# Two loads and a few casts moved behind a named neighbour, in a hybrid decoder block

## The chip, the cores and the metric

The program runs on one core of a Trainium2 chip. The metric is the device time of one execution in microseconds (us), as the median of several runs; the profile is one further execution, taken by the hardware profiler. The core has a matrix engine (TensorE; PE in the profile, with PEld for its weight loads), VectorE (DVE), ScalarE (ACT), GpSimd (POOL) and SyncE (SP), which here does nothing but issue DMA transfers. Each engine works through its instructions in the order written in the program and waits on semaphores for the others.

## The reference

One decoder block on x of 1024 tokens by 1024 channels: a state-space branch and a forgetting-attention branch read one normalised input; they are gated and joined; then cross-attention into 256 memory tokens, and a gated feed-forward network (FFN).

```python
u = rms_norm(h, norm_mix); proj = u @ w_in            # u_ssm, q, k, v, f_logit, gate_logits
y_ssm = gelu(s5_ssm(u_ssm, ...))
glu_a, glu_b = split(y_ssm @ w_glu);  out_a = glu_a * sigmoid(glu_b)
att   = forgetting_attention(q, k, v, f_logit + b_forget)    # 8 heads of 64, causal
out_b = att @ w_fox_o
h = h + (gate_a * out_a + gate_b * out_b) @ w_mix_out
h = h + memory_cross_attention(rms_norm(h), rms_norm(mem), w_mem_q, w_mem_kv, w_mem_o)
f_a, f_b = split(rms_norm(h) @ w_ffn_in)                     # hidden width 2816
h = h + (silu(f_a) * f_b) @ w_ffn_out
return rms_norm(h, norm_final)
```

## The kernel before, in words

Every matrix product is made of three: an operand is split into a high part (`hi`, a cast on ACT, L177) and the rest (`lo`, a subtraction, mostly on DVE, L178), and hi x hi, hi x lo and lo x hi are added up in one PSUM bank. A weight thus goes through a raw slot (a DMA), a cast and a subtraction before TensorE can use it. There are two raw slots (`raw`) and four pairs of slots for the parts (`whi`, `wlo`). `B.wload` and `B.wblock` do all three steps. The large products of the tail use seven block products instead of eight (the numbers 1 to 7 in the code), so their weights are also summed before they are split.

The program is written as straight-line Python. A scheduler then sets the order in which each engine's instructions stand, by readiness, by the order written and by free slots of the pools, so an instruction may stand well ahead of its place in the code. `B.behind(ins)` (and `tc.issue_after`) holds the instructions of its block that run on the engine of `ins` behind `ins` in that engine's order. It orders the queue; it adds no wait of its own. A queue such as SP's is worked off in order: an issue that waits for a slot holds all issues behind it.

Three places matter.

**The attention (`Fox.run`).** Eight heads, each of 12 units (`scores`, `values_hi`, `values_lo`). Beside the units of head h run: the row maxima of head h+1 (`row_max`, and `max_row`, which stores them by DMA at L1722 into the row `hb`), the projection of head h+2 (`pro[h + 2].parts`, 16 pieces; for the last head 8 pieces beside head 5 and 8 beside head 6), and the load and split of the weights for head h+3 (`load`, L1652 and L1653, from `w_in`, placed behind the broadcast `spread` of the reciprocals; `split`, placed behind an exponential). So the last w_in load is issued in head 4. When a head is done, `finish` moves its denominators (`rc`, `rd_d`, `rb`) through DRAM and `divide` applies them in the next head. From the time that TensorE no longer reads the tiles of `uT`, the SSM branch's output is loaded into their slots (`load_y`, L1810). In the last head (7) the first four gated units are computed beside the units, as `filler`: for each j a load of its weights (`Glu.load`, two DMAs of 256 KB from `wg_d`, a copy of w_glu in DRAM, and a split of 128x1024), then two products (`value`).

**The first part of the tail (`stage_tail`).** For j = 0 to 7 the second half of a gated unit is finished (`glu.rest`, which loads the gate `ga`, L1211) and the attention's product for j-3 is made, multiplied by the gate `gb` and added (`fox_part`; the gate load is `load`, L555, the multiplication L587). `ga`, `gb` and others share five slots `half`; the units' outputs `sg` and others share five slots `tmp`. For j = 0 to 3 `sg` is then stored to `am_d` (L595) and its slot is free when that store has landed. `ahead(j, ...)` prepares the weights of the first two FFN tiles long before they are due: `fetch` loads two raw halves of 512 KB (`wpr`, L652), `plain`, `sums`, `seventh` and `rest` split them and store the parts to `w_d`. `ahead1` is the second tile; its raw halves use `tmp` slots, and its steps are called one by one in `side`, between the block products of the output projection (`mix_mm`, L627).

**The end of the FFN.** The first FFN product runs over 22 tiles j; for each, `start`, `middle` and `end` make the block products (`prod`, L977). `middle` ends with the copy `c1` (L998) of the bank `b1`, to which `end` then adds product 3. The second product (`o_mm`, L1114) takes its operands in pairs from DRAM: `o_get(m)` loads two halves (`or`, L1097 and L1103) and splits them, into a `whi`/`wlo` pair for m < 4 and into other slots (`oh`, `ol`) afterwards. The first four are asked for before the last `end`, three more behind it.

The order that the scheduler gives is shown below, since the code alone does not tell it.

Of the kernel before, what the change touches and what calls it, by code (L numbers as in the profile page):

```python
# [22 lines left out]
NT = 8  # L23
GRP = 32
NH = 8
# [41 lines left out]
def f32(ap):  # L67
    return ap.bitcast(F32)
# [471 lines left out]
def stage_tail(B, big, s2, sh, x, glu, aT, gate_d, kv_d, sums_d, w_fox_o, w_mix_out, g_mq, w_mem_q, w_mem_o, g_ffn,  # L540
               w_ffn_in, w_ffn_out, g_fin, out):
    nc, V, A, G, T, S, small, ident = B.nc, B.V, B.A, B.G, B.T, B.S, B.small, B.ident
# [9 lines left out]

    def load(src, name):
        t_ = sh.half(name)
        S.dma_start(t_, src)  # L555
        return t_


# [131 lines left out]
    ahead0, ahead1 = ahead(0, lambda name, dt=F32: slot(dt, name)), ahead(1, tmp)  # L690
# [43 lines left out]
    def mix_s4(kk):  # L734
        y = s2.tile([P, D], F32, tag=("xs", "gbc")[kk], bufs=1, name="s4")
        S.dma_start(y, s3_d[kk])
        for k in range(2):
            give("S4", slot, 2 * kk + k, y[:, 512 * k:512 * k + 512])

    side = [ahead1[0]] + [lambda kk=kk: mix_s4(kk) for kk in range(2)] + ahead1[1:2] + [lambda: None] + ahead1[2:3] + \  # L740
        [lambda: None] + ahead1[3:]
    mix_weights(6)
    for i in range(4):
# [245 lines left out]
    def middle(j):  # L989
        b1 = ev[j, "b1"]  # L990
        b3 = ev[j, "b3"] = B.bank("pv")
        prod(j, 6, b1, False)
        a1 = ev[j, "a1"] = sh.half("a1")
        A.copy(a1, b1)
        prod(j, 7, b3, True)
        prod(j, 5, b1, False)
        c1 = ev[j, "c1"] = sh.half("c1")
        A.copy(c1, b1)  # L998
        V.scalar_tensor_tensor(out=c1, in0=c1, scalar=-1.0, in1=b3, op0=ALU.mult, op1=ALU.subtract)

    def end(j):
# [89 lines left out]
    ops, Hf = {}, {}  # L1091
    ssq = small.tile([P, 2 * NT], F32, name="ssq", bufs=1)

    def o_get(m):
        n, p = seq[m]
        r_ = slot(name="or")
        S.dma_start(r_[:, :512], c_d[n, p])  # L1097
        if n < 4:
            j, c = 2 * p + (n > 1), 512 * (n > 2)
            src = w_ffn_out[j * P:(j + 1) * P, c:c + 512]  # L1100
        else:
            src = t_d[n, p]
        S.dma_start(r_[:, 512:], src)  # L1103
        hl = wpair(0) if m < 4 else (bslot(F32R, "oh"), bslot(F32R, "ol"))
        B.split(*hl, r_)
        ops[m] = hl

    def o_mm(m, i):
# [26 lines left out]
            S.dma_start(out[t * P:(t + 1) * P, cs], Hf[t][:, cs])  # L1135

    for m in range(4):
        o_get(m)
    end(NF - 1)
    for m in range(4, AHEAD):  # L1140
        o_get(m)
    gated(NP - 1)
    out_sums(NP - 1, 1)
    gfin = B.bcast_gain(s2, g_fin)
# [386 lines left out]
class Fox:  # L1531
# [90 lines left out]
    def setup(self):  # L1622
        fp, G = self.fp, self.B.G
        self.hb = [[self.sh.tmp("hb", F32R) if i == 0 else fp.tile([P, L], F32R, name=f"hb{s}") for s in range(4)]
                   for i in range(2)]
        for K1, K2, Q1, Q2 in self.hb:
            G.memset(f32(K1[64:69, :]), 1.0)
            G.memset(f32(Q1[64:69, :]), -1.0)

        self.tri = fp.tile([P, 512], F32, name="tri")  # L1630
        G.memset(self.tri, 0.0)
        G.affine_select(out=self.tri[:, 384:512], in_=self.tri[:, 384:512], pattern=[[-1, P]], compare_op=ALU.is_ge,
                        fill=NEG, base=0, channel_multiplier=1)
        self.trk = fp.tile([P, P], F32, name="trk")
        G.memset(self.trk, 0.0)
        G.affine_select(out=self.trk, in_=self.trk, pattern=[[1, P]], compare_op=ALU.is_ge, fill=NEG, base=0,
                        channel_multiplier=-1)
        self.pj, self.mc, self.pvs, self.num, self.rb, self.raw = {}, {}, {}, {}, {}, {}
        self.hi_todo, self.lo_todo = [], []

    def project(self, h):

# [71 lines left out]
    def max_row(self, h):  # L1714
        B = self.B
        mc = self.mc.pop(h)
        B.V.tensor_tensor(out=mc[:, 0, :], in0=mc[:, 0, :], in1=mc[:, 1, :], op=ALU.max)
        pm = B.bank("misc")
        B.T.transpose(pm[0:NT, 0:P], mc[:, 0, :], B.ident)
        mr = B.small.tile([NT, P], F32R, tag="mr", bufs=1, name="mr")  # L1720
        B.V.tensor_scalar(out=mr, in0=pm[0:NT, 0:P], scalar1=-1.0, scalar2=None, op0=ALU.mult)
        B.S.dma_start(f32(self.hb[h % 2][2][68:69, :]).rearrange("o (a b) -> o a b", a=NT), f32(mr))  # L1722

    def scores(self, h, qc, kt):
        B, fp = self.B, self.fp
# [72 lines left out]
    def run(self, y_d, yT, aT, w_glu, w_d, filler):  # L1798
        B, fp, S = self.B, self.fp, self.B.S
        self.aT = aT  # L1800
        self.prepare_v()
        for t in range(NT):
            self.values_of_v(1, t)
        self.log_forget()
        self.setup()

        def load_y(k, h):

            for i, dst in enumerate(yT.rhs(k, h)):
                S.dma_start(f32(dst).rearrange("p (t c) -> p t c", t=4),  # L1810
                            y_d[k, i, 4 * h:4 * h + 4].rearrange("t p c -> p t c"))

        def load_att(k):
            for h in range(2):
                for i, dst in enumerate(aT.rhs(k, h)):
                    S.dma_start(f32(dst), self.att_d[i, k * P:(k + 1) * P, 512 * h:512 * h + 512])

        pro = [self.project(h) for h in range(NH)]
        for h in range(2):
            loaded = pro[h].load()  # L1820
            pro[h].split()

        with B.tc.issue_after(loaded.ins):
            for k in range(4):
                S.dma_start(w_d[k].rearrange("(m g) c -> m g c", g=8),
                            w_glu[k * P:(k + 1) * P].rearrange("(g m) c -> m g c", m=16))
        for f in pro[0].parts[:8] + pro[0].evac[:1] + pro[0].parts[8:] + pro[0].evac[1:]:
            f()
        self.cumulate()
        for t in range(4):  # L1830
            self.values_of_v(0, t)
        for h in range(2):
            self.gate_rows(h)
        for f in pro[1].parts[:4]:
            f()
        weave(pro[1].parts[4:8] + pro[1].evac[:1] + pro[1].parts[8:], self.row_max(0))
        copied = pro[1].evac[1]()
        self.values_of_v(0, 4)
        self.max_row(0)
        pro[2].load()  # L1840
        pro[2].split(copied)
        pro[3].load()
        for t in range(5, 7):
            self.values_of_v(0, t)
        units = [(qc, kt) for qc in range(2) for kt in range(4 * qc + 4)]
        for h in range(NH):
            side = {i: [] for i in range(12)}
            late = h == NH - 2
            if late:
                for i, f in enumerate(pro[h + 1].parts[8:]):  # L1850
                    side[i // 2].append(f)
                side[3].append(pro[h + 1].evac[1])
            if h + 1 < NH:
                for i, f in enumerate(self.row_max(h + 1)):
                    side[(RSLOT_LATE if late else RSLOT)[i]].append(f)
                side[9].append(lambda: self.max_row(h + 1))
            if h + 2 < NH:
                n = 8 if h + 3 == NH else 16
                for i, f in enumerate(pro[h + 2].parts[:n]):
                    side[i if n == 8 else PSLOT[i]].append(f)  # L1860
                side[9].append(pro[h + 2].evac[0])
                if n == 16:
                    side[11].append(pro[h + 2].evac[1])
            if h + 3 < NH:
                side[9].append(lambda: pro[h + 3].split(self.exp))
            if h > 0 and h + 3 < NH:
                side[5].append(lambda: pro[h + 3].load(self.spread))
            if h == 0:
                side[0].append(lambda: self.values_of_v(0, 7))
            if late:  # L1870
                for k in range(8):
                    side[4 + k].append(lambda k=k: load_y(k // 2, k % 2))
            if h == NH - 1:
                for k in range(3):
                    side[6 + k].append(lambda k=k: load_att(k))
                for i, f in enumerate(filler):
                    side[i * 12 // len(filler)].append(f)
            for i, u in enumerate(units):
                self.scores(h, *u)
                for f in side[i]:  # L1880
                    f()
                if len(self.hi_todo) > 2:
                    self.values_hi()
                if len(self.lo_todo) > 1:
                    self.values_lo()
                if h and i == 4:
                    with B.tc.issue_after(self.mark.ins):
                        self.divide(h - 1)
        while self.hi_todo:
            self.values_hi()  # L1890
        while self.lo_todo:
            self.values_lo()
        self.divide(NH - 1)
# [29 lines left out]
```

## Time and profile before

| | |
|---|---|
| median of three runs | 1577.26 us (1577.14, 1577.26, 1582.96) |
| the profiled execution | 1575.91 us |
| its span, first to last instruction | 1574.2 us |
| mean granted TensorE clock | 0.992 |
| TensorE busy | 1524.9 us, 97% of the span |
| VectorE, ScalarE, GpSimd busy | 1055.2, 680.2 and 239.3 us |
| HBM read and written | 175.04 and 83.20 MB |

The times of a profile count from the start of the span. A row of a timeline gives the start, the duration, the engine, the line and the operation, with the tile written left of the arrow and the tiles read right of it; in square brackets stands how long the engine was idle just before, and what ended that. SPq and ACTq are rows of DMA issues, not of transfers. A wait row gives the total, the number of times and the longest. A row by stretch gives the busy time of each engine with the number of instructions, the granted TensorE clock as a share of full speed, the mean busy share of the DMA engines, and GB/s.

### The profile page before, as it was taken

Reading aid. Unit: us, or ns where it says so; the run is one execution under the profiler, and the core shown is the slowest. Engines: PE = TensorE matmul, PEld = TensorE weight load, DVE = VectorE, ACT = ScalarE, POOL = GpSimd, SP = SyncE. Lnnn points to the kernel's source line nnn. Section 1 sums busy time; section 2 is a strip of 40 time slices with the busy share of each in tenths; the row PEclk is TensorE's granted clock in tenths of the full one; section 3 lists DMA queues with packets and bytes.
Section 4 is the critical chain, followed back from the end, with each engine's and each line's share of the span. In section 5 each row is a group of like instructions: output and inputs, shape, how many; then the busy total and the mean of one; then the engine's idle time right before and its main releaser. Section 6 shows DMA issues by size and latency. Waiting matters only on the chain.

```text
span 1574.2 us, 20451 instructions
## 1 busy us (share of the span) xinstructions
PE 1524.9 (97%) x7261; PEld 1251.0 (79%) x7261; DVE 1055.2 (67%) x1893; ACT 680.2 (43%) x1203; POOL 239.3 (15%) x323
## 2 busy tenths in 40 slices
PE   7899999999999899999999989999999999999997
PEld 6688888898776678778788778888888888788886
DVE  5937755554777776678756687677777776565555
ACT  6523343423665653343445564333333333354342
POOL 3145342200211122210002100000000000000001
PEclk9999999999999999999999999999999999999999
DMA  8655657642124637767431186444445444896642
GB/s 255 140 134 101 185 160 154 186 131 27 35 43 69 165 113 220 245 215 265 162 107 54 67 304 243 162 154 154 158 158 164 160 159 152 286 385 217 198 148 107
DMA packets 202586, 257.66 MB, mean 164 GB/s; under 512 B 35994, under 2 KB 127034, under 8 KB 201972
## 3 DMA queue, kind: packets, MB, share of 16 engines
q1 hardware_dynamic: 195860, 240.62, 51.0%
q10 hardware_dynamic: 6624, 15.73, 2.6%
q8 instruction: 57, 0.93, 0.2%
q14 instruction: 45, 0.37, 0.1%
HBM read 175.04 MB, written 83.20 MB: 164 GB/s over the span
## 4 chain that ended last, share of the span: by engine, by line
PE 77%; DVE 8%; DMA 7%; ACT 3%; issue 2%; POOL 2%; SPq 1%; DVEq 0%; POOLq 0%; ACTq 0%
PE mm L977 15%; PE pv L977 8%; PE mm L167 6%; PE mm L168 6%; PE mm L169 6%; PE mm L1114 5%; PE sc L977 4%; PE sc L1114 4%; PE pv L1114 3%; PE sc L167 2%; PE sc L169 2%; PE sc L168 2%; PE misc L1114 2%; DMA gb<-gate_d 1%; PE mm L627 1%
## 5 line engine op out<-in xcount | busy, mean ns | idle before, releaser
L178 DVE TENSOR_TENSOR wlo<-raw,whi 128x1024 fp32r<-128x1024 f32 (+2 forms) x126 | 133.9, 1064 | 107.2 <-ACT whi L177 106.8
L177 ACT CAST whi<-raw 128x1024 fp32r<-128x1024 f32 (+2 forms) x127 | 115.9, 915 | 136.5 <-PE mm L168 35.8
L167 PE MATMUL mm<-uh,whi 128*128 128x512 f32 x344 | 137.6, 400 | 3.1 <-ACT whi L177 3.0
L178 DVE TENSOR_TENSOR ol<-or,oh 128x1024 fp32r<-128x1024 f32 x73 | 89.3, 1224 | 70.3 <-ACT oh L177 69.2
L168 PE MATMUL mm<-ul,whi 128*128 128x512 f32 x344 | 135.7, 395 | 0.0
L169 PE MATMUL mm<-uh,wlo 128*128 128x512 f32 x344 | 135.1, 393 | 0.5 <-DVE wlo L178 0.5
L177 ACT CAST oh<-or 128x1024 fp32r<-128x1024 f32 x73 | 76.9, 1053 | 103.0 <-PE mm L1114 33.3
L1009 POOL TENSOR_TENSOR g<-a,c 128x512 f32<-128x512 f32 x22 | 35.6, 1617 | 392.6 <-ACT a L1008 354.1
L167 PEld LDWEIGHTS mm<-uh,whi 128*128 128x128 f32 x344 | 65.4, 190 | 15.5 <-ACT whi L177 3.5
L196 POOL TENSOR_TENSOR r<-ms,mhalf 128x1 f32<-128x1 f32 (+1 forms) x30 | 19.4, 650 | 379.6 <-DVE ms L192 347.2
L169 PEld LDWEIGHTS mm<-uh,wlo 128*128 128x128 f32 x344 | 65.1, 189 | 14.8 <-DVE wlo L178 1.5
L1742 POOL TENSOR_TENSOR pl<-pf,ph 128x512 fp32r<-128x512 f32 (+1 forms) x32 | 39.5, 1236 | 243.8 <-DVE ph L1741 197.3
L168 PEld LDWEIGHTS mm<-ul,whi 128*128 128x128 f32 x344 | 65.4, 190 | 11.0
L1739 ACT ACTIVATE pf<-sc 128x512 f32<-128x512 f32 (+1 forms) x96 | 46.5, 491 | 48.1 <-DVE sc L1735 28.3
L977 PE MATMUL pv<-S3h,we 128*128 128x512 f32 x176 | 58.1, 389 | 0.0
L1745 DVE TENSOR_TENSOR pl<-pf,ph 128x512 fp32r<-128x512 f32 (+2 forms) x64 | 35.7, 558 | 10.1 <-ACT ph L1744 9.3
L1114 PE MATMUL mm<-oh 128*128 128x512 f32 x106 | 41.2, 389 | 0.0
L1114 PE MATMUL mm<-ol,oh 128*128 128x512 f32 x106 | 41.2, 389 | 0.0
L1114 PE MATMUL mm<-oh,ol 128*128 128x512 f32 x106 | 41.2, 389 | 0.0
L167 PE MATMUL mm<-yh,whi 128*128 128x512 f32 x104 | 40.9, 393 | 0.0
L167 PE MATMUL sc<-uh,whi 128*128 128x512 f32 x104 | 40.8, 392 | 0.0
L169 PE MATMUL mm<-yh,wlo 128*128 128x512 f32 x104 | 40.6, 390 | 0.0
(689 smaller groups left out, 4559.7 us busy)
## 6 DMA issues: line engine op xcount, KB each, us to landing
or<-c_d SPq DMA_DIRECT2D x77, 256.0 KB
wo<-in_w_ffn_out_dram SPq DMA_DIRECT2D x22, 512.0 KB
c_d<-g SPq DMA_DIRECT2D x44, 256.0 KB
t_d<-wo SPq DMA_DIRECT2D x44, 256.0 KB
or<-t_d SPq DMA_DIRECT2D x44, 256.0 KB
raw<-in_w_ffn_in_dram SPq DMA_DIRECT2D x20, 512.0 KB
rawb<-in_w_ffn_in_dram SPq DMA_DIRECT2D x20, 512.0 KB
raw<-in_w_in_dram SPq DMA_DIRECT2D x18, 512.0 KB
```

The source lines that it names most:

```text
L167: T.matmul(ps, lh, rh, start=first, stop=False)
L168: T.matmul(ps, lh, rl, start=False, stop=False)
L169: T.matmul(ps, ll, rh, start=False, stop=last)
L177: self.copied = self.A.copy(hi, src)
L178: (self.G if pool_lo else self.V).tensor_sub(lo, src, f32(hi))
L196: self.G.tensor_tensor(out=r, in0=v, in1=self.mhalf[:, 0:n], op=ALU.pow)
L977: T.matmul(ps, l_[:, k, :], r_, start=first and k == 0 and i == 0, stop=k == 3 and i == 2, skip_group_check=True)
L1009: G.tensor_mul(g[:, 512:], a1, c1)
L1114: T.matmul(ps, l_[:, gi], r_[:, 512:], start=n < 3 and p == 0 and k == 0 or n == 7 and p == 0 and k == 0, stop=p == NP - 1 and k == 2, ski ...
L1739: self.exp = A.activation(pf[:, off:], ps[:, off:], AF.Exp)
L1742: G.tensor_sub(pl[:, off:], pf[:, off:], f32(ph[:, off:]))
L1745: V.tensor_sub(pl[:, off:], pf[:, off:], f32(ph[:, off:]))
```

## The change

Three edits, each of which puts something that the scheduler had placed early behind an instruction by name. No instruction is added or removed.

1. In `Fox.run` the first `filler` step, `Glu.load(0)`, is called behind `maxed[6]`, the DMA that stores the row maxima of head 6. Both its DMAs are on SP, so they are what is held.
2. In `stage_tail` the call of `ahead1[0]` (`fetch`, two DMAs on SP) is put behind `sh.loaded`, the last gate load that `load` has issued by then.
3. At the end, `o_get` puts its split behind `ev["last"]`, the copy `c1` of the last tile, for m > 1. The cast is on ACT as `c1` is, so it is what is held; the loads are not.

```diff
     def load(src, name):
         t_ = sh.half(name)
-        S.dma_start(t_, src)
+        sh.loaded = S.dma_start(t_, src)
         return t_
...
+    def ahead1_fetch():
+        with B.behind(sh.loaded):
+            ahead1[0]()
+
-    side = [ahead1[0]] + [lambda kk=kk: mix_s4(kk) for kk in range(2)] + ahead1[1:2] + [lambda: None] + ahead1[2:3] + \
+    side = [ahead1_fetch] + [lambda kk=kk: mix_s4(kk) for kk in range(2)] + ahead1[1:2] + [lambda: None] + ahead1[2:3] + \
...
-        A.copy(c1, b1)
+        ev["last"] = A.copy(c1, b1)
...
-    def o_get(m):
+    def o_get(m, behind=None):
...
-        B.split(*hl, r_)
+        with B.behind(behind):
+            B.split(*hl, r_)
...
     for m in range(4):
-        o_get(m)
+        o_get(m, ev["last"] if m > 1 else None)
     end(NF - 1)
     for m in range(4, AHEAD):
-        o_get(m)
+        o_get(m, ev["last"])
...
-        B.S.dma_start(f32(self.hb[h % 2][2][68:69, :]).rearrange("o (a b) -> o a b", a=NT), f32(mr))
+        self.maxed[h] = B.S.dma_start(f32(self.hb[h % 2][2][68:69, :]).rearrange("o (a b) -> o a b", a=NT), f32(mr))
...
-                for i, f in enumerate(filler):
+                def first():
+                    with B.behind(self.maxed[NH - 2]):
+                        filler[0]()
+
+                for i, f in enumerate([first] + filler[1:]):
                     side[i * 12 // len(filler)].append(f)
```

What this does to the order, at the places that the prediction speaks of. The lines of the changed program stand up to nine higher, since lines were added: L1652, L1722, L1775 and L1791 of before are L1657, L1727, L1780 and L1796, L1211 is L1216, and L994, L998 and L1008 are L998, L1002 and L1012 (so the copy `c1` is L998 before and L1002 now).

SP's queue in head 4, from the last w_in load on, before; `raw_5654` is the first gated unit's raw slot, `rc` a head's denominators, `yh` and `yl` the SSM branch's output:

```order
L1652 DMA raw_4992<-in_w_in_dram 128x8x64
L1653 DMA raw_4992<-in_w_in_dram 128x8x64
L153 DMA raw_5654<-wg_d_2972 128x4x128 x2
L1791 DMA att_d_80<-ahi_4967 64x1024
L1791 DMA att_d_80<-alo_4968 64x1024
L1687 DMA hb_3273<-cum_d_81 2x1024
```

and now:

```order
L1657 DMA raw_4992<-in_w_in_dram 128x8x64
L1658 DMA raw_4992<-in_w_in_dram 128x8x64
L1796 DMA att_d_80<-ahi_4967 64x1024
L1796 DMA att_d_80<-alo_4968 64x1024
L1692 DMA hb_3273<-cum_d_81 2x1024
```

The two loads have left the place behind the w_in loads; the stores of the head's output follow at once. The same queue where they now stand, before; `raw_5738`, `raw_5823` and `raw_5907` are the second, third and fourth unit:

```order
L1722 DMA hb_3275<-mr_5343 1x8x128
L153 DMA raw_5738<-wg_d_2972 128x4x128 x2
L153 DMA raw_5823<-wg_d_2972 128x4x128 x2
L1687 DMA hb0_3277<-cum_d_81 2x1024
L1775 DMA rc_5453<-num_5193 128x1x8
L1688 DMA hb2_3279<-cum_d_81 2x1024
L153 DMA raw_5907<-wg_d_2972 128x4x128
```

and now:

```order
L1727 DMA hb_3275<-mr_5343 1x8x128
L153 DMA raw_5654<-wg_d_2972 128x4x128 x2
L153 DMA raw_5738<-wg_d_2972 128x4x128 x2
L1692 DMA hb0_3277<-cum_d_81 2x1024
L1780 DMA rc_5453<-num_5193 128x1x8
L1693 DMA hb2_3279<-cum_d_81 2x1024
L153 DMA raw_5823<-wg_d_2972 128x4x128
```

Each unit's load stands in the place that the next one's had. The fourth unit's goes behind the row maxima of head 7, and its cast and subtraction into head 7.

SP's queue in the tail around the last store to `am_d`, before; `wpr_7026` and `wpr_7027` are the second FFN tile's raw halves:

```order
L595 DMA am_d_5999<-sg_5940 128x1024
L652 DMA wpr_7026<-in_w_ffn_in_dram 128x8x128
L1211 DMA ga_6663<-gate_d_79 128x512
L1211 DMA ga_6666<-gate_d_79 128x512
L555 DMA gb_6688<-gate_d_79 128x512
L555 DMA gb_6711<-gate_d_79 128x512
```

and now:

```order
L595 DMA am_d_5999<-sg_5940 128x1024
L1216 DMA ga_6663<-gate_d_79 128x512
L1216 DMA ga_6666<-gate_d_79 128x512
L555 DMA gb_6688<-gate_d_79 128x512
L555 DMA gb_6711<-gate_d_79 128x512
```

The first half has moved to where the second stood, behind the last `gb`, and the second goes behind the next load of `sums_d`.

ACT's order around the last copy `c1`, before:

```order
L177 CAST whi_12128<-or_12125 128x1024
L177 CAST whi_12135<-or_12132 128x1024
L177 CAST whi_12142<-or_12139 128x1024
L1008 ACTIVATE a1_11949<-a1_11949 128x512
L994 COPY a1_12091<-mm_12009 128x512
L177 CAST oh_12189<-or_12186 128x1024
L177 CAST oh_12196<-or_12193 128x1024
L998 COPY c1_12117<-mm_12009 128x512
L177 CAST whi_12149<-or_12146 128x1024
```

and now:

```order
L177 CAST whi_12128<-or_12125 128x1024
L177 CAST whi_12135<-or_12132 128x1024
L1012 ACTIVATE a1_11949<-a1_11949 128x512
L998 COPY a1_12091<-mm_12009 128x512
L1002 COPY c1_12117<-mm_12009 128x512
L177 CAST whi_12142<-or_12139 128x1024
L177 CAST whi_12149<-or_12146 128x1024
L177 CAST oh_12189<-or_12186 128x1024
```

The copy has passed the casts of the operands m = 2, 4 and 5. On TensorE three matmuls of the second product (L1114), which stood ahead of product 3 of the last tile, stand behind products 3 and 4 instead. On VectorE the subtractions follow their casts; the one for `wpr_7026` moves ahead of the last gate product of `fox_part(7)`.

More of the change, by code (lines that the diff above doesn't have):

```diff
@@ L1638, in setup @@
         self.pj, self.mc, self.pvs, self.num, self.rb, self.raw = {}, {}, {}, {}, {}, {}
-        self.hi_todo, self.lo_todo = [], []
+        self.hi_todo, self.lo_todo, self.maxed = [], [], {}
     def project(self, h):
```

## The prediction

> **What bounds the kernel now.** I read the busy times, then who TensorE waits for, then busy time and granted clock by stretch around the three places of the change, and last the engines and SP's queue there in order of time.
>
> ```profile
> PE 1524.9 (97%) x7261; PEld 1251.0 (79%) x7261; DVE 1055.2 (67%) x1893; ACT 680.2 (43%) x1203; POOL 239.3 (15%) x323
> ...
> PE pv L167 <- DVE gb L587: 4.1, 3, 3.0
> PE mm L167 <- ACT whi L177: 3.0, 1, 3.0
> PE sc L1732 <- ACT pf L1739: 2.9, 4, 1.9
> ...
> PE mm L977 <- ACT c L998: 1.0, 1, 1.0
> PE mm L169 <- DVE wlo L178: 0.5, 1, 0.5
> ```
>
> TensorE is busy for 97% of the span, so only its idle time and its slow clock are to be had. In the waits (total, times, longest) the reader sees three that belong to the three edits: 3.0+0.5 us for a cast weight in the attention, 3.0 us for a gate product in the tail, 1.0 us for an evacuation at the end.
>
> ```profile
> 508.00:521.00 13.00, 9.41 (x40) 6.87 (x39) 5.88 (x14) 7.43 (x14) 0.00 (x0) 0.87 0.42 118
> ...
> 529.00:541.00 12.00, 10.13 (x41) 6.93 (x39) 8.80 (x20) 5.83 (x10) 1.45 (x2) 0.86 0.81 201
> 541.00:558.00 17.00, 15.41 (x74) 10.47 (x73) 13.84 (x36) 13.33 (x27) 3.32 (x3) 1.00 0.38 111
> ...
> 688.00:700.00 12.00, 8.96 (x33) 6.91 (x32) 7.61 (x11) 2.46 (x4) 2.49 (x2) 0.86 0.81 271
> 700.00:720.00 20.00, 20.00 (x89) 16.55 (x89) 17.71 (x28) 7.19 (x11) 0.00 (x0) 1.00 0.64 215
> ...
> 1348.00:1352.00 4.00, 2.99 (x13) 2.15 (x12) 1.68 (x2) 3.25 (x4) 0.00 (x0) 1.00 0.96 289
> ```
>
> The columns are stretch, length, busy time of PE, weight load, DVE, ACT and POOL, granted clock, DMA share, GB/s. From 508 to 521 PE idles 13.00-9.41 = 3.59 us and the clock of 0.87 costs 13 x 0.13 = 1.69 us more: 5.3 us. From 688 to 700 it is 3.04 and 12 x 0.14 = 1.68: 4.7 us. At 1348 it is 1.01 us at full clock. From 529 to 541 stand another 1.87 + 1.68 = 3.6 us that no edit names.
>
> **Edit 1, the first gated unit's weights.** Two loads (256 KB each, w_glu's copy into a raw slot) leave their place behind head 4's w_in loads and go behind the row maximum of head 6; one cast and one subtraction of 128x1024 move with them, nothing is added.
>
> ```profile
> 470.52 0.57 SPq L1653 DMA_DIRECT2D raw<-in_w_in_dram  x1
> 475.95 0.47 SPq L1791 DMA_DIRECT2D att_d<-ahi  x1
> ...
> 495.38 0.57 SPq L1653 DMA_DIRECT2D raw<-in_w_in_dram  x1
> 496.00 9.20 SPq L153 DMA_DIRECT2D raw<-wg_d  x2
> 505.29 2.52 SPq L1791 DMA_DIRECT2D att_d<-ahi  x1
> ...
> 539.97 2.08 SPq L153 DMA_DIRECT2D raw<-wg_d  x4
> ```
>
> ```profile
> 481.45 1.05 ACT L177 CAST whi<-raw 128x1024 fp32r<-128x1024 f32 x1
> ...
> 505.75 0.58 ACT L1680 CAST hb<-mm 64x512 fp32r<-64x512 f32 x1
> 511.47 1.04 ACT L177 CAST whi<-raw 128x1024 fp32r<-128x1024 f32 x1 [5.14 <-DMA raw<-in_w_in_dram]
> ...
> 563.07 1.20 DVE L178 TENSOR_TENSOR wlo<-raw,whi 128x1024 fp32r<-128x1024 f32 x1
> ```
>
> ```profile
> 512.57 0.50 PE L167 MATMUL mm<-uh,whi 128*128 128x512 f32 x1 [3.03 <-ACT whi L177]
> ```
>
> SP is held 9.20 us by the two issues, and the w_in load ahead of them lands only at 511.47, 16.1 us after its issue. In the head before, with no such neighbour, the cast follows the issue by 481.45-470.52 = 10.9 us and waits for no DMA. By that row the load is there at 506.3, which is when ACT is free (505.75+0.58): the cast starts 5.1 us earlier, at 506.4, ends at 507.4, and the lo part, 1.20 us on DVE, at about 508.7, before PE runs dry at 512.57-3.03 = 509.5. So the idle 3.59 us go, and with them the slow stretch. Bounds: 0 (the small pieces of w_in are slow by themselves) to 5.3 us. I take 5.3, since the row of the head before is the same load under the same order. Behind it the att_d stores and the cum_d loads also leave SP up to 4 us sooner.
>
> What it costs later: the unit's weights now take the place of the second unit's, which go to the third's, and so on; the fourth's move to head 7.
>
> ```profile
> 546.46 1.05 ACT L177 CAST whi<-raw 128x1024 fp32r<-128x1024 f32 x1
> ...
> 558.08 0.50 PE L167 MATMUL mm<-yh,whi 128*128 128x512 f32 x1
> ```
>
> The cast at 546.46 is the second unit's and becomes the first's; PE first reads it at 558.08, so there are some 10 us of cover. The fourth unit's cast and subtraction (1.05 and 1.20 us) come into head 7, where PE has the units' products as side work; I charge 0.3 us, between 0 and 1.05 (one cast in front of an exponential, unhidden). SP there meets one wait more: the fifth unit's load stands ahead of the store of head 6's reciprocals and waits for the fourth's subtraction. The division that reads them stands behind none of PE's waits above, so I charge nothing; uncovered it costs the 1.20 us.
>
> **Edit 2, the second FFN tile's raw weights.** Of two loads of 512 KB the first leaves SP's queue ahead of the gate loads; both go behind the last gate load. Their casts and sums stay the same in number.
>
> ```profile
> SPq L652 <- DMA am_d<-sg: 3.1, 1, 3.1
> ...
> 684.41 0.34 SPq L595 DMA_DIRECT2D am_d<-sg  x1
> 687.88 0.37 SPq L652 DMA_DIRECT2D wpr<-in_w_ffn_in_dram  x1
> 688.35 0.99 SPq L1211 DMA_DIRECT2D ga<-gate_d  x2
> 689.40 6.30 SPq L555 DMA_DIRECT2D gb<-gate_d  x5
> ...
> 704.11 0.39 SPq L652 DMA_DIRECT2D wpr<-in_w_ffn_in_dram  x1
> ```
>
> ```profile
> 661.38 7.12 DMA gb<-gate_d
> ...
> 674.41 4.26 DMA gb<-gate_d
> ...
> 694.18 0.69 DVE L587 TENSOR_TENSOR gb<-gb,pv 128x512 f32<-128x512 f32 x1 [4.23 <-DMA gb<-gate_d]
> ```
>
> ```profile
> 694.93 0.62 PE L167 MATMUL pv<-ath,whi 128*128 128x512 f32 x1 [3.04 <-DVE gb L587]
> ```
>
> SP waits 3.1 us at L652 until the store of am_d has landed, because the load wants that slot, and the gate loads queue behind it. Without it they are issued 688.35-684.8 = 3.5 us sooner, the first gb at 685.9. Landing 4.26 to 7.12 us later it is there at 690.2 to 693.0; PE runs dry at 694.93-3.04 = 691.9, the product takes 0.69 us, so the stall falls to between 0 and 1.8 us. I take 0, by the 4.26 row (the 512 KB of the moved load are no longer in flight beside it): 4.7 us won, of 1.2 to 4.7. The moved load starts about where the second one stood (704.11 less the gain), and its cast stands no earlier in ACT's row; the DVE is 89% busy from 700 to 720 and one subtraction of 1.20 us now stands ahead of the last gate product: I charge half of it, 0.6 us, between 0 and 1.2.
>
> **Edit 3, the second product's operands.** The casts of the third to seventh operand go behind the last evacuation c1, which passes three of them in the row; no work is added.
>
> ```profile
> 1343.47 1.06 ACT L177 CAST oh<-or 128x1024 fp32r<-128x1024 f32 x1 [0.55 <-PE pv L977]
> 1348.75 1.05 ACT L177 CAST oh<-or 128x1024 fp32r<-128x1024 f32 x1 [4.23 <-DMA or<-in_w_ffn_out_dram]
> 1349.71 0.58 ACT L998 COPY c<-mm 128x512 f32<-128x512 f32 x1
> ...
> 1347.58 0.39 PE L1114 MATMUL sc<-whi 128*128 128x512 f32 x1
> 1350.34 0.50 PE L977 MATMUL mm<-S4h,wdh 128*128 128x512 f32 x1 [1.01 <-ACT c L998]
> ```
>
> ACT stood 4.23 us on a load with the copy behind it. The bank is complete at 1347.58, so the copy runs from about 1347.8 to 1348.4, and PE goes from its four product matmuls (to 1348.5) straight on to S4: 1350.34-1348.5 = 1.8 us, less the three matmuls that move behind it (20.00 us over 89 from 700 to 720: 0.23 each): 1.2 us, of 0 to 1.3. The postponed casts have PE's 24 matmuls of the two last products (5.4 us) as cover.
>
> **Sum.** 5.3 + 4.7 + 1.2 - 0.3 - 0.6 = 10.3 us. The profiled execution took 1575.91 us (span 1574.2), 1.35 us under the median of 1577.26; against its own time that is 1565.6, as a median 1567.0.
>
> **Two rules against it.** The half-speed stretch behind the gaps of 3.03 and 3.04 us is in the rows above (0.87 and 0.86). The Trainium skill ("TensorE: Matmul & The Clock Gate", Part 1) says the clock halves after at least one idle window of about 3.4 us. Neither gap is that long and the clock fell all the same, so the trace decides; by the rule the slow stretches have another cause and stay, and the sum would be 10.3-3.4 = 6.9 us (R4). The load of 496.00 was read 62 us later, and two loads beside it paid. The Trainium skill ("DMA: Bandwidth & Descriptors", Rules for kernel authors) says to issue a DMA early and wait late; by it edits 1 and 2 win nothing, and the sum is 1.2-0.9 = 0.3 us (R7). The trace agrees that distance hides a load, and shows what that costs its neighbours in the queue.
>
> **Rivals.**
> - R1, w_in is slow by itself: 5.3 us stay, 1572.3. For: it is cut into pieces of 64 columns. Against: the head before.
> - R2, the gate loads come no sooner, or the stall moves to the next gate product: 4.7 us stay, 1571.7.
> - R3, heads 5 and 6 give it back: from 541 to 558 DVE and ACT are 81% and 78% busy and PE already idles 1.6 us; if these two bound the heads, 5 us go, 1572.
> - R4, the gaps go but the slow clock stays (1.7 + 1.7 us): 1570.4. Against: full clock behind them (700 to 720).
> - R5, the unnamed stall at 529 to 541 (the 1.9 us of L1732) goes too, since the first transfer of its chain now stands one load earlier on SP and ACT has one cast less ahead of it: 3.6 us more, 1563.4.
> - R6, slower: the issues jam in their new place as at 496.00. Four at 4.6 us are 18.4 instead of 2.08, 16.3 lost, since head 7's cum_d rows queue behind them; the next pair costs another 9.20-1.04 = 8.2. That is 1567.0+24.5 = 1591.5; from 10.3 us of jam on it is slower than before. Against: four such issues took 2.08 us in that very place.
> - R7, moving loads back gains nothing anywhere: 1577.0. Against: both waits name what the moved loads hold up.
>
> **Chances.** The forecast (own range 1563.5 to 1569.4) 0.52; R5 0.08; R1 0.09; R2 0.08; R3 0.10; R4 0.05; R7 0.03; R6 0.05. Half a per cent is 7.9 us, about what a measurement of this kernel tells from no change. Faster by more: forecast and R5, 0.60; within it: R1 to R4 and R7, 0.35; slower: 0.05. The range 1562.5 to 1573.0 leaves out R6, R7 and the far ends of the others.
>
> **What would show it.** After: no wait of PE for whi near 510 and SP's w_in issue followed directly by att_d; the gb product at about 685 with no PE gap and a clock of 1.00; c1's copy within 0.3 us of its last matmul. Wrong would be a w_in load that still lands 16 us after issue, a new wait of PE between 540 and 600, or gate loads that wait on SP for another slot.

## The result and the profile after

| | before | after |
|---|---|---|
| runs, median (lowest to highest) | 9, 1578.66 us (1575.97 to 1582.96) | 9, 1571.31 us (1564.84 to 1574.28) |
| profiled execution, span | 1575.91, 1574.2 us | 1564.84, 1563.1 us |

The ratio is 0.9949 (95% interval 0.9932 to 0.9965), 8.0 us faster; a second set of runs (`after_again`, below) gave 0.9934 (0.9920 to 0.9948). Both profiles stand at the fast end of their runs: before's 1575.91 lies below all nine of before, after's is the fastest of its nine. The 11.1 us between the two are more than the runs show; part of the reason is a finding of its own at the end.

Who TensorE waits for, after (total, times, longest; `pf` are the exponentials of the attention, `c` is the copy `c1`):

```profile
PE sc L1737 <- ACT pf L1744: 3.3, 4, 2.3
...
PE pv L167 <- DVE gb L587: 1.0, 1, 1.0
...
PE mm L167 <- ACT whi L177: 0.8, 1, 0.8
...
PE mm L169 <- DVE wlo L178: 0.5, 1, 0.5
```

The wait for `gb` of 3.0 is gone (the 1.0 that stays is at 632, no place of an edit), that for `c` is gone altogether, that for `whi` fell from 3.0 to 0.8, and the one for `pf`, which no edit names, stayed. By stretch, with the columns of before:

```profile
508.00:521.00 13.00, 11.57 (x56) 8.30 (x56) 8.75 (x26) 8.95 (x19) 0.74 (x1) 1.00 0.38 113
529.00:541.00 12.00, 9.88 (x43) 7.33 (x44) 8.72 (x23) 5.69 (x12) 1.28 (x1) 0.86 0.84 223
680.00:700.00 20.00, 20.00 (x90) 16.56 (x89) 18.18 (x26) 7.96 (x13) 3.00 (x2) 1.00 0.80 249
```

TensorE's 3.59 idle us from 508 to 521 are 1.43 now and the clock holds at 1.00; from 680 to 700 there is no idle time left; 529 to 541 is about as it was (2.12 us idle, 1.87 before, clock 0.86 again).

Edit 1: SP's issues, then ACT, then TensorE, whose last row here is the matmul that stood at 558.08 before:

```profile
494.54 0.58 SPq L1657 DMA_DIRECT2D raw<-in_w_in_dram  x1
495.17 0.57 SPq L1658 DMA_DIRECT2D raw<-in_w_in_dram  x1
500.64 1.45 SPq L1796 DMA_DIRECT2D att_d<-ahi  x1
502.23 2.23 SPq L1796 DMA_DIRECT2D att_d<-alo  x1
```

```profile
508.98 1.05 ACT L177 CAST whi<-raw 128x1024 fp32r<-128x1024 f32 x1 [2.87 <-DMA raw<-in_w_in_dram]
```

```profile
510.08 0.51 PE L167 MATMUL mm<-uh,whi 128*128 128x512 f32 x1 [0.78 <-ACT whi L177]
...
554.46 0.50 PE L167 MATMUL mm<-yh,whi 128*128 128x512 f32 x1
```

The att_d stores now stand next in the queue, yet ACT gets the load only at 508.98, 13.8 us after its issue at 495.17, not the 10.9 that I had taken. Even the stores' own issues take 1.45 and 2.23 us. At 554.46 TensorE is 3.6 us ahead of before.

Edit 2, on SP and DVE, and then edit 3, on ACT and TensorE:

```profile
678.33 0.34 SPq L595 DMA_DIRECT2D am_d<-sg  x1
678.77 1.17 SPq L1216 DMA_DIRECT2D ga<-gate_d  x2
679.99 8.23 SPq L555 DMA_DIRECT2D gb<-gate_d  x5
```

```profile
684.69 0.68 DVE L587 TENSOR_TENSOR gb<-gb,pv 128x512 f32<-128x512 f32 x1
```

```profile
1337.93 0.59 ACT L1002 COPY c<-mm 128x512 f32<-128x512 f32 x1 [4.04 <-PE mm L981]
1338.41 2.00 ACT L177 CAST whi<-or 128x1024 fp32r<-128x1024 f32 x2
```

```profile
1338.64 0.44 PE L981 MATMUL mm<-S4h,wdh 128*128 128x512 f32 x1
```

The gate loads are issued 1.66 us behind the am_d store instead of 4.99, and the product waits for no DMA. The copy c waits for nothing but its matmuls, the casts stand behind it, and TensorE goes on without a gap.

### The profile page after: what moved, and what is told of

Read it like the earlier page. It is cut to its first block, busy times and chain, and to the rows that moved or that the text cites. A ratio compares the mean times of both kernels' runs of the same rounds, so it can differ in the third digit from the quotient of the medians.

```text
span 1563.1 us, 20461 instructions
## 1 busy us (share of the span) xinstructions
PE 1521.1 (97%) x7261; PEld 1249.2 (80%) x7261; DVE 1055.7 (68%) x1893; ACT 679.3 (43%) x1203; POOL 239.5 (15%) x323
## 4 chain that ended last, share of the span: by engine, by line
PE 84%; DVE 6%; DMA 4%; ACT 3%; issue 1%; POOL 1%; SPq 0%; DVEq 0%; POOLq 0%; ACTq 0%
PE mm L981 15%; PE pv L981 8%; PE mm L167 7%; PE mm L168 7%; PE mm L169 7%; PE mm L1119 5%; PE sc L981 4%; PE sc L1119 4%; PE pv L1119 3%; PE sc L169 3%; PE sc L167 3%; PE sc L168 3%; PE misc L1119 2%; PE mm L627 1%; PE pv L167 1%
## 5 line engine op out<-in xcount | busy, mean ns | idle before, releaser
L1750 DVE TENSOR_TENSOR pl<-pf,ph 128x512 fp32r<-128x512 f32 (+2 forms) x64 | 35.1, 549 | 10.1 <-ACT ph L1749 9.3
```

The lines of the kernel that those rows point to most:

```text
L1750: V.tensor_sub(pl[:, off:], pf[:, off:], f32(ph[:, off:]))
```

## The three edits alone

Each run is the kernel before with one edit, beside after once more, on one chip with 26 runs of before.

**e1_only**

```diff
+                def first():
+                    with B.behind(self.maxed[NH - 2]):
+                        filler[0]()
```

> The kernel before with edit 1 alone. Theory A (the head-7 w_in load is slow by itself, and the moved loads cost it only part of its delay): the w_in load lands some 13 to 14 us after its issue instead of 16.1, TensorE waits about 0.8 us for whi and 0.5 for wlo, the clock stays at 1.00 from 508 to 521, and the later heads run 3.6 to 3.9 us sooner; time 3 to 4 us under before (ratio about 0.9975). Theory B (my prediction's): lands within 10.9 us, no wait, 5.0 us under before (0.9968). Rival C: head 7 gives it back, within 1 us of before (1.000).

**e2_only**

```diff
+        with B.behind(sh.loaded):
+            ahead1[0]()
```

> The kernel before with edit 2 alone. Theory: SP issues the gate loads some 3.5 us sooner against the store of am_d, the 3.0 us wait for gb and the slow stretch behind it go, time 4.1 to 4.7 us under before (ratio about 0.9972). Rival: the stall only moves to another gate product or to the second tile's weights (wpl), then at most 1.5 us are won (0.999 to 1.000) and the wait for gb stays near 4 us in total.

**e3_only**

```diff
-        o_get(m)
+        o_get(m, ev["last"] if m > 1 else None)
```

> The kernel before with edit 3 alone. Theory: TensorE's 1.0 us wait for c goes and nothing else moves, time 1.0 to 1.3 us under before (ratio 0.9992), which the runs cannot tell from no change; the trace shows it. Rival: the postponed casts make a new wait for oh or ol of up to 1 us and the time is that of before.

**after_again** (no edit)

> The changed kernel once more, beside the three edits on one chip. If the edits are independent its distance from before is the sum of the three, 8.5 to 10 us (ratio 0.9937 to 0.9946). If a slow stretch of the clock (3.4 us at half speed, 1.7 us lost) comes and goes from run to run with where a gap falls, the runs scatter by some multiples of 1.7 us and their mean clock moves with their time, by 0.0011 for each; then the profiled run, not the mechanism, is what made 11.1 us out of 7.4. Rival: the scatter has nothing to do with the clock, and runs of equal time have clocks that differ.

| | median us | ratio to before (95%) |
|---|---|---|
| e1_only, 12 runs | 1577.50 | 0.9977 (0.9964 to 0.9991) |
| e2_only, 12 runs | 1576.82 | 0.9973 (0.9958 to 0.9988) |
| e3_only, 8 runs | 1576.18 | 0.9983 (0.9968 to 0.9997) |
| after_again, 6 runs | 1569.37 | 0.9934 (0.9920 to 0.9948) |

In parts of a thousand the singles win 2.3, 2.7 and 1.7, together 6.7; all three at once win 6.6 here and 5.1 in the first set. As far as intervals of about 1.5 on either side can tell, the edits add up. Theory A of e1_only fits (the load's last piece ends 13.7 us after its issue, TensorE waits 1.0 and 0.5 us), e2_only came out as its theory has it, and in e3_only the wait for `c` is gone without a new one for `oh` or `ol`. Times of whole runs scatter by more than an edit is worth, so the size of each is better read at its place. The table takes each matmul of a profile, subtracts the start of the same matmul in before, and gives the median over 20 us from the time named (of before; negative is ahead):

| | 500 | 520 | 680 | 700 | 1300 | 1360 |
|---|---|---|---|---|---|---|
| after | -0.2 | -4.0 | -4.4 | -9.3 | -9.8 | -11.1 |
| after_again | 4.1 | 2.1 | 1.7 | -3.2 | -3.7 | -4.9 |
| e1_only | 0.9 | -2.6 | -1.5 | 0.4 | -1.6 | 2.9 |
| e2_only | 4.0 | 3.4 | 1.9 | -3.1 | -1.1 | -1.0 |
| e3_only | 2.7 | 2.9 | 1.0 | 2.4 | 1.8 | 0.6 |

An edit's worth is the step between two columns. Edit 1 wins 3.8, 2.0 and 3.5 us (500 to 520 in after, after_again and e1_only; the 2.0 has a slow stretch of the clock at 517 in it, 1.7 us), edit 2 4.9, 4.9 and 5.0 (680 to 700 in after, after_again and e2_only), edit 3 1.3, 1.2 and 1.2 (1300 to 1360 in after, after_again and e3_only). Without their edit, the same places lose time in some profiles against this one of before, so the stalls have no fixed size. The waits of e1_only show it for the two places that it leaves alone:

```profile
PE pv L167 <- DVE gb L587: 4.8, 3, 3.8
PE mm L977 <- ACT c L998: 3.9, 1, 3.9
```

```profile
1350.04 1.04 ACT L177 CAST oh<-or 128x1024 fp32r<-128x1024 f32 x1 [6.91 <-DMA or<-in_w_ffn_out_dram]
1350.99 0.58 ACT L998 COPY c<-mm 128x512 f32<-128x512 f32 x1
```

ACT stood 6.91 us on the load of an operand here, 4.23 in before, and TensorE waited 3.9 us for the copy c instead of 1.0; in e2_only, which lacks edit 3 as well, it waited 1.1. So edit 3 takes away a stall of 1 to 4 us in these three profiles, which fits its 2.7 us by the runs (interval 0.5 to 5.1).

## The slow load: addresses or place?

It was open what the 13.8 us were due to: the stores and the place in head 4, or the load itself. Its 2048 pieces (DMA packets of 256 bytes in the trace) took 12.3 us from the first to the last in after and 12.5 in e1_only, but 14.8, 14.0 and 14.4 with the gated unit's loads beside them (before, e2_only, e3_only); the loads for heads 4, 5 and 6 took 5.6 to 7.3 in all of these. So the neighbours cost about 2 us, and the rest is there without them.

**swap67**

```diff
-            src = lambda c: self.w_in[:, c + h * DH:c + (h + 1) * DH].rearrange(...)
+            g = {6: 7, 7: 6}.get(h, h)
+            src = lambda c: self.w_in[:, c + g * DH:c + (g + 1) * DH].rearrange(...)
```

> The changed kernel with the w_in columns of heads 6 and 7 exchanged (head 6 works with head 7's q and k weights and the other way round; the work, the order and the sizes stay). In six profiles so far the 2048 pieces of the head-7 load took 12.3 to 14.8 us from first to last, those of heads 4, 5 and 6 took 5.6 to 7.3. Theory A (the addresses): now the load issued in head 3 takes 12 us or more and the one issued in head 4 about 6, lands by 504, and the cast there waits for no DMA. Theory B (the place in the program: what else runs in head 4): the load issued in head 4 stays at 12 to 13 us and the cast still waits about 3 us.

The program exchanges these columns and nothing that belongs to them (values, gate rows, output), so heads 6 and 7 compute something else; it has one run, of 1569.71 us, and serves for its trace alone. By stretch (the last two columns are the DMA engines' share and GB/s), after with the head-6 load at 471 and the head-7 load at 497, then swap67 with the two exchanged:

```profile
471.30:475.30 4.00, 4.00 (x22) 2.95 (x20) 3.23 (x6) 2.46 (x5) 0.64 (x1) 1.00 0.91 80
497.00:504.00 7.00, 7.00 (x33) 5.13 (x33) 6.44 (x14) 4.35 (x7) 1.29 (x1) 1.00 0.44 22
```

```profile
475.00:482.00 7.00, 7.00 (x33) 4.96 (x32) 6.89 (x14) 4.85 (x9) 1.28 (x1) 1.00 0.47 28
500.00:504.00 4.00, 4.00 (x22) 3.08 (x21) 3.10 (x7) 2.45 (x5) 0.46 (x1) 1.00 0.84 83
```

```profile
486.20 1.05 ACT L177 CAST whi<-raw 128x1024 fp32r<-128x1024 f32 x1 [2.81 <-DMA raw<-in_w_in_dram]
...
510.10 1.05 ACT L177 CAST whi<-raw 128x1024 fp32r<-128x1024 f32 x1
```

The slow rate went with the columns: 12.1 us for the load in head 3, 6.5 for the one in head 4, and ACT's wait moved one head forward. Theory A holds: it is the addresses. What about them is slow no run tells (a row of w_in has 4104 floats, 16,416 bytes).

**w7early** issues that load a head earlier.

```diff
-            if h > 0 and h + 3 < NH:
+            if 0 < h < 4:
                 side[5].append(lambda: pro[h + 3].load(self.spread))
+            if h == 3:
+                side[6].append(lambda: pro[7].load(self.stored))
```

> The changed kernel with the head-7 w_in load issued one head earlier, behind the stores of head 2's output (about 478 instead of 494.5), into the raw slot that edit 1 left free; nothing else moves. Theory (the rest of edit 1's stall is this load's own slowness): lands by about 492, 14 us ahead of its cast, no wait of ACT or TensorE for it; 1.3 to 1.7 us won, 3.4 where the clock also dropped: ratio 0.9920 to 0.9930 beside 0.9934 to 0.9949 of the changed kernel. Rival: the row maxima of head 4 (hb<-mr, issued at 484) now queue behind its pieces and TensorE waits for them at 490 by up to 8 us: slower than the changed kernel.

(`stored` is the att_d store of head 2.) The ratio is 0.9965 (0.9953 to 0.9977), so it won less than after (0.9934 and 0.9949). SP's rows, and TensorE's longest wait in the attention:

```profile
481.50 0.89 SPq L1658 DMA_DIRECT2D raw<-in_w_in_dram  x1
486.02 2.81 SPq L1692 DMA_DIRECT2D hb<-cum_d  x1
488.93 1.75 SPq L1727 DMA_DIRECT2D hb<-mr  x1
```

```profile
PE sc L1737 <- DMA hb<-mr: 5.1, 1, 5.1
```

That is the rival: there is no wait for w_in any more, but one of 5.1 us for the 4 KB of row maxima behind it. Here the slow load costs whoever is next in the queue.

**rot** works the heads in another order, so that these columns are loaded early, with some 50 us of cover.

```diff
+            g = h ^ 4
-            src = lambda c: self.w_in[:, c + h * DH:c + (h + 1) * DH].rearrange(...)
+            src = lambda c: self.w_in[:, c + g * DH:c + (g + 1) * DH].rearrange(...)
...
-                for k in range(3):
-                    side[6 + k].append(lambda k=k: load_att(k))
+                for i, k in enumerate((0, 2, 3)):
+                    side[6 + i].append(lambda k=k: load_att(k))
```

and `h ^ 4` for `h` likewise in `cum_d`, `vh`, `vl`, `att_d` and `aT`.

> The changed kernel with the heads worked in the order 4, 5, 6, 7, 0, 1, 2, 3: the slow head-7 columns of w_in are now loaded fourth (at about 354), 50 us ahead of their cast, and the columns of head 3 are the last. Nothing else changes, the result is the same. Theory (these columns' addresses are slow, and with cover that costs nothing): the load at 494 takes 5.6 to 7.3 us like those of heads 4 to 6, ACT's cast and TensorE wait for no w_in in any head; 1.3 to 1.7 us won on the changed kernel, 3.4 where the clock also dropped: ratio to before 0.992 to 0.994. Rival: other columns that were hidden until now (0 to 3) are slow too, the wait comes back in one of the last four heads, and the ratio is that of the changed kernel, 0.9934 to 0.9949.

The ratio is 0.9920 (0.9906 to 0.9934), the median 1567.25 us.

```profile
510.25 1.05 ACT L177 CAST whi<-raw 128x1024 fp32r<-128x1024 f32 x1 [1.39 <-DMA raw<-in_w_in_dram]
```

TensorE waits for no w_in in any head. The rival had a point: the load that is last now (head 3) takes 10.8 us, most of it for its second thousand pieces, the k columns, and ACT still waits 1.39. By the measure of the table above, rot wins 5.2 us on before from 500 to 520 and swap67 5.8, where edit 1 alone won 3.5 to 3.8: with a load that comes in time, the place gives the 5.3 us of the prediction.

## The stall at 529 that no edit names

**ybehind**

```diff
-                    side[4 + k].append(lambda k=k: load_y(k // 2, k % 2))
+                    side[4 + k].append(lambda k=k: load_y(k // 2, k % 2, self.spreads[NH - 4]))
```

(`load_y` puts its two DMAs behind that instruction; `spreads[h]` is the broadcast `rb` of head h.)

> The changed kernel with the 16 loads of the SSM branch's output (y_d to yh and yl, 256 KB each) held behind the broadcast rb of head 4's reciprocals. Theory (the stall at 529 to 541 comes from these loads: the small store rd_d lands 4.5 us after issue behind them instead of 1.4, so ACT's cast ahi waits 2.7 us on the division with the exponentials behind it): rb is issued 1.4 us after rd_d, the wait of TensorE for pf and the slow stretch there go, 1.5 to 4 us won. Rival A: the loads now reach into head 5's chain (542 to 548) and make the same stall 26 us later, nothing won. Rival B: the first gated unit waits for yh or for its weights near 554, up to 5 us lost.

SP in after, SP in ybehind, then ybehind's waits of TensorE and one row of ACT:

```profile
519.30 0.36 SPq L1782 DMA_DIRECT2D rd_d<-rc  x1
...
523.79 0.47 SPq L1784 DMA_DIRECT2D rb<-rd_d  x1
```

```profile
525.36 0.35 SPq L1782 DMA_DIRECT2D rd_d<-rc  x1
526.80 0.47 SPq L1784 DMA_DIRECT2D rb<-rd_d  x1
```

```profile
PE mm L167 <- ACT whi L177: 4.9, 3, 2.9
...
PE sc L1737 <- ACT pf L1744: 0.8, 2, 0.5
```

```profile
557.96 1.04 ACT L177 CAST whi<-raw 128x1024 fp32r<-128x1024 f32 x1 [4.60 <-DMA raw<-wg_d]
```

The cause is shown: without y loads around it, rd_d is followed by rb after 1.44 us instead of 4.49, and the wait for `pf` falls from 2.3 to 0.5 at its longest. But the scheduler then put the gated unit's weights behind the y loads, and TensorE waits for those: 3.7 us won from 520 to 540, 2.9 lost again by 560. The ratio of 0.9944 (0.9930 to 0.9957) is that of after, and Rival B came true.

**w7early_ybehind** has both edits.

> Both of the last two together. If both theories hold, 3 to 7 us under the changed kernel (ratio to before 0.989 to 0.992). If the y loads only move the stall, the ratio is that of the early w_in load alone, 0.992 to 0.993.

The ratio is 0.9949 (0.9933 to 0.9965): the program has both new waits, 4.8 us for `hb` and 3.6 for `whi`.

**rdact** takes the two small steps off SP's queue.

```diff
-        S.dma_start(self.rd_d[h].rearrange("(p c) -> p c", c=NT), rc)
+        q = B.A if h == NH - 4 else S
+        q.dma_start(self.rd_d[h].rearrange("(p c) -> p c", c=NT), rc)
...
-        self.spread = S.dma_start(rb, ...)
+        self.spread = q.dma_start(rb, ...)
```

> The changed kernel with two transfers of head 4 (the store rd_d and the broadcast rb of the reciprocals) issued by ACT, on its own DMA queue, instead of SP's, where they stand among the 16 loads of y. Theory (rd_d lands late because it queues behind the y loads in SP's queue): rd_d lands 1.4 to 2 us after its issue instead of 4.5, ACT's cast ahi at 529 waits under 1 us, the wait for pf of 1.4 to 2.6 us at 529 to 541 goes with its slow stretch: 1.4 to 4 us won on the changed kernel. Rival A (it is the shared DMA engines that are full, not the queue): rd_d lands as late as before, nothing won. Rival B: ACT's own issue of rb waits for the landing of rd_d with the exponentials behind it, and the stall stays, 2 us or more.

The ratio is 0.9954 (0.9936 to 0.9971). With the new head order as well, it is **rot_rdact**:

> Both of the last two. If both theories hold, the gains add: 3 to 6 us under the changed kernel, ratio to before 0.990 to 0.9925. If ACT's queue does not help, the ratio is that of the new head order alone.

The ratio is 0.9955 (0.9941 to 0.9970), against 0.9920 (0.9906 to 0.9934) for the order alone on the same chip: the two steps on ACT's queue cost 5.5 us. ACT in rdact, then DVE and TensorE:

```profile
524.90 0.33 ACTq L1783 DMA_DIRECT2D rd_d<-rc  x1
...
528.88 0.50 ACTq L1785 DMA_DIRECT2D rb<-rd_d  x1
529.48 0.62 ACT L1749 CAST ph<-pf 128x512 fp32r<-128x512 f32 x1 [2.25 <-DMA rd_d<-rc]
```

```profile
534.72 1.22 DVE L1791 TENSOR_TENSOR num<-num,rb 64x1024 f32<-64x1024 f32 x1 [2.96 <-DMA rb<-rd_d]
```

```profile
537.07 0.79 PE L1710 MATMUL mm<-hb 68*128 68x512 f32 x1 [3.72 <-DVE mc L1712]
```

On ACT's queue the 4 KB store still needs 3.98 us (4.51 in rot_rdact), so SP's queue was not what it waited in (Rival A), and ACT stood 2.25 us for it with the exponentials behind (Rival B). The loss came with it: DVE waited 2.96 us for rb, and TensorE 3.72 us for `mc`, a row maximum that DVE makes after that; in rot_rdact the waits for this `mc` are 6.8 us in all, in rot 0.6. The Trainium skill ("DMA: Bandwidth & Descriptors", Queues, rings and completion order) says that a DMA's semaphore write lands only after all earlier writes of the same DMA engine, across its queues. The trace agrees: 3.98 us beside 4.49.

**rot_y2** is rot with less in flight when rd_d is issued.

```diff
+                    side[4 + k].append(lambda k=k: load_y(k // 2, k % 2, self.spreads[NH - 4] if 1 <= k < 2 else None))
```

> The new head order (4 to 7, then 0 to 3), and of the 16 y loads only the second pair is held behind the broadcast rb of the fifth worked head, so that 5 of them instead of 6 stand ahead of the store rd_d and none between rd_d and rb; the first gated unit's weights keep a place ahead of the next head's chain. Theory (rd_d waits for what is in flight on the shared DMA engines when it is issued): rb is issued some 3 us after rd_d instead of 3.9, ACT's cast ahi waits 1.0 to 1.5 us instead of 2.4, the wait for pf falls to about 1 us: 1 us won on the new order alone, 2.7 where the clock had dropped; ratio to before 0.990 to 0.992. Rival: the gated units' weights or the next head's chain come later for it and nothing is won, 0.992 to 0.994.

SP in rot, then SP and ACT in rot_y2:

```profile
520.56 0.38 SPq L1784 DMA_DIRECT2D rd_d<-rc  x1
...
524.49 0.47 SPq L1786 DMA_DIRECT2D rb<-rd_d  x1
```

```profile
520.44 0.34 SPq L1784 DMA_DIRECT2D rd_d<-rc  x1
523.22 0.47 SPq L1786 DMA_DIRECT2D rb<-rd_d  x1
```

```profile
528.13 1.05 ACT L177 CAST ahi<-num 64x1024 fp32r<-64x1024 f32 x1 [0.42 <-DVE num L1792]
```

rb follows after 2.78 us, in rot after 3.93, and ACT waits 0.42 us there instead of the 2.37 of rot and the 2.67 of after. From 520 to 560 rot_y2 wins 3.6 us on before, rot 1.1, one profile each and no slow stretch of the clock there in either. The median is 1560.62 us beside 1576.55 of before on that chip; the ratio is 0.9918 (0.9891 to 0.9945), wide since one of the six runs took 1570.40. So the gain shows at its place, but against rot's 0.9920 the runs decide nothing. And rot itself is not clear of after by the runs: its interval meets those of after's 0.9934 and 0.9949.

## What the prediction had right and wrong

- **The sum.** The forecast was 10.3 us. The three places give 9.6 to 10.1 together, without after_again's 500 to 520, where the clock dropped; the runs give 8.0 in the first set and 10.4 in the second (0.0066 x 1579.7). The median of 1571.31 lies in the whole range, but above the forecast's own (to 1569.4); by time alone R1 to R4 (1570.4 to 1572.3) would fit as well, and only the traces tell them apart. That the sum comes so close is in part luck: edit 1 was put 1.5 to 1.8 us too high, and the charges of 0.3 and 0.6 us, which no profile shows, made up for half of it.
- **Edit 1, 5.3 less 0.3.** This is the term that failed: measured 3.5 to 3.8. The step "the head before is the same load under the same order" was wrong, since the columns of head 7 are slow (12.3 us instead of 5.9 for head 6). R1 was right about the load and wrong about the price: the moved neighbours did cost it 2 us, and without them TensorE's gaps shrink from 3.6 to 1.3 us in after, where the clock held; it held in e1_only too and fell in after_again. The give-back of 0.3 is not shown: after loses 0.4 us from 520 to 540, at the stall that no edit names, and after_again wins 1.5 there. From 540 to 620 after's lead stays at 3.6, so head 7 takes nothing; e1_only and after_again lose 1.3 to 1.4 us between 540 and 560, but so do e2_only and e3_only (1.1 to 1.2), which lack edit 1.
- **Edit 2, 4.7 less 0.6.** 4.9 to 5.0: the gate loads came the 3.3 us sooner that I had put at 3.5, the product stands at 684.69 (forecast 685), and the 0.6 us for one subtraction on DVE did not appear. e2_only loses 2.5 us again by 900, with a wait of 2.4 us for the residual `h` at 769; after and after_again, which have the same edit, wait 0.4 and 0.3 us for it, so I take that for scatter.
- **Edit 3, 1.2.** 1.2 to 1.3 against this profile; 1 to 4 us over several, a spread that one profile cannot show. (20.00 us over 89 matmuls are 0.22 each, not 0.23; the term stays.)
- **The rivals.** R5 was wrong: the chain stood behind the y loads, not behind the first gated unit. R2 did not come: the gate loads came sooner, and no other gate product took the stall over. Nor did R3, by the leads above, or R6: four issues took 2.08 us in the new place again. R7 was wrong: moving a load back did gain, at its neighbours. R4 was right in one point: the clock fell again at 517 in after_again, though the gaps there were 1.2 and 0.5 us.

## What to carry to other kernels

When one load is late, compare the rate of its pieces with those of its like before blaming the neighbours in the queue; a load slow by its addresses is best moved to where it has more cover than it takes (12 us here) and no urgent transfer behind it. The small store here, whose landing releases a chain, was late beside large loads on either queue (4.49 and 3.98 us, 1.44 without them); keep such loads away from the time between its issue and its landing. Read the worth of a 1 us edit from the same instruction in two profiles, and take its sign from several runs.

## What the hardware showed that I had not expected

**The clock drops on a grid.** All slow stretches last 3.41 us or a multiple (but for the last of each profile, which the end cuts off), and start on a grid of 3.41 us that runs through the whole execution. Stretches of one grid step and the next, for before, after and after_again (TensorE's busy time is the second number, its clock the third from the end):

```profile
510.80:514.21 3.41, 1.12 (x3) 0.48 (x3) 1.62 (x3) 2.68 (x4) 0.00 (x0) 1.00 0.29 103
514.21:517.62 3.41, 3.37 (x12) 2.77 (x12) 3.14 (x5) 1.60 (x6) 0.00 (x0) 0.51 0.05 14
```

```profile
507.31:510.73 3.42, 2.64 (x13) 1.50 (x11) 0.77 (x2) 1.64 (x3) 0.00 (x0) 1.00 0.39 136
510.73:514.14 3.41, 2.88 (x17) 2.23 (x17) 2.95 (x7) 2.18 (x6) 0.00 (x0) 1.00 0.07 21
```

```profile
513.70:517.11 3.41, 1.72 (x8) 1.15 (x9) 2.23 (x5) 3.19 (x6) 0.00 (x0) 1.00 0.06 23
517.11:520.53 3.42, 3.42 (x12) 2.64 (x11) 1.40 (x3) 2.00 (x4) 0.00 (x0) 0.50 0.31 85
```

After's gaps (0.78 and 0.53 us) fell into two steps and the clock held; those of after_again (1.2 and 0.5 us) fell into one, which left it half busy, and the next step ran at half speed. Over the 14 profiles, without the last steps of each, I counted full-speed steps by TensorE's busy share: under 0.4 the next was slow in 43 of 43, from 0.4 to 0.5 in 15 of 17, from 0.5 to 0.7 in 16 of 93, above 0.7 in none of 6065. The Trainium skill ("TensorE: Matmul & The Clock Gate", Part 1) has the free-running window of 3413 ns, and there the trace agrees; it says "idle window", and here half busy was enough, so the measurement decides.

**And so a stall has two prices.** Where a gap falls on the grid differs between the two profiles of one kernel, a slow step costs up to 1.7 us (half of 3.41), and that part of the scatter shows: over 157 runs of before and of the kernels above (each against the mean of its own) a run is 1.08 us longer for each 0.001 that its mean clock is lower, and the spread falls from 2.5 to 1.8 us (standard deviation) when that is taken off. One slow step lowers the mean clock by 0.0011, so at its full price it would be 1.6 us for each 0.001 (an estimate from these numbers); part of the slow steps seems to be paid less than in full, which no run here tests. The rest of the scatter is unexplained.
